# Up projection in one-bank PSUM tiles, with the next pair's seven products set among the last three up tiles

## The chip, the cores and the metric

The kernel runs on one core of one Trainium2 chip. The metric is the device time of one execution in microseconds (us); lower is better. All matrix products are float32 products made of three float32r (fp32r) products: every weight tile is cast to a high part `whi`, and the rest `wlo` is what the cast left; the left operand is split in the same way.

## The reference, cut to what matters

One decoder layer on x of 256 tokens by 2048 features: RMSNorm, two token mixers and an output projection, then a gated MLP. Only the MLP's first product and what follows it are touched:

```python
h = rmsnorm(x, norm_ffn_w[l])
gate, up = jnp.split(jnp.einsum('bsd,df->bsf', h, w_up[l]), 2, axis=-1)   # w_up: 2048 x 11264
gate = causal_dwconv(gate, conv_ffn_w[l]) + conv_ffn_b[l]                  # 3 taps over the tokens
x = x + jnp.einsum('bsf,fd->bsd', jax.nn.gelu(gate, approximate=False) * up, w_down[l])
return rmsnorm(x, norm_final_w)
```

## The kernel before, in words

**The up projection (the loop over c at lines 1334 to 1373).** The 5632 gate columns and the 5632 up columns are cut into 11 pairs of 512 columns. A pair c has four quarters of results, each 128 tokens by 512 columns and one PSUM bank large: `bank[col, t]`, col 0 the gate and 1 the up columns, t the half of the tokens. Four banks are taken as two tiles of two banks from the pool `psm`: (0,0) and (1,0) share a tile, (1,1) and (0,1) share the other.

The sum over the 2048 input features goes in eight chunks of 256 (`kp`). A **plain step** (col, kp) loads one weight tile of 256 by 512 and makes 12 matmuls of 128x512 with it: two token halves, two 128-row slices, and three products each (`products`, L1286 to L1290: high by high, low of the left by high, high of the left by low of the weight). Below, g0 to g5 are the plain steps of the gate column of a pair in the order of kp, u0 to u5 those of the up column. Pair 0 has eight of each. In pairs 1 to 10 the first two chunks are left to a **seven-product scheme** (Strassen's in Winograd's form) over 2x2 blocks: `split_parts` (L1298 to L1328) makes the products T1, 11, T2, 21, T3, 22, T4 of six matmuls each in place of eight. T1 goes into a bank `y` of its own and is copied to SBUF as `own` (L1317); 11 goes into (0,1) and is copied into (0,0) (L1319); T2 is added to (0,1); VectorE writes (1,0) = (0,1) + own (L1322); 21 is added to (0,0); T3 is added to (0,1); VectorE writes (1,1) = (0,1) + own (L1326); 22 is added to (1,0) and T4 to (0,1). Then the plain steps add to all four.

**Order before.** Pair c begins with its seven products; between them stand the transposes of pair c-1's results (`turned`, L332, eight for the gate, eight for the up half, into tiles of `psg`). Then come the plain steps in the order g0, g1, u0, g2, u1, g3, u2, g4, u3, g5, u4, u5. A scheduler that the framework runs at build time may move instructions on every engine within what the data allow.

**Weights.** `weights()` (L158) hands out the next tile and calls `begin` (L231) for the third one after it: the DMA on SyncE's queue (L170, four buffers `raw`), the cast on ScalarE (`whi`, L244) and the rest on VectorE (`wlo`, L252, "the split" below). `whi` and `wlo` have three buffers, so the cast of a tile waits for the last matmul that reads the high part three tiles back. For the seven products four quarter tiles are loaded into the buffer `quad` (`quad_load`, L184, at the earliest when the last pair's T4 has been split) and combined in place on VectorE (`up_sum`, L190: one sum ahead of T1, one behind the split of T1, two behind that of T2).

**What follows a pair.** ScalarE copies the four quarters to SBUF (`e`, L1366 for the gate with a scale, L1368 for the up half), TensorE transposes them, and `gate_part` (L1249: ScalarE L1256, eight VectorE instructions L1261, Gelu L1265) and `up_part` (L1269: L1274, L1281, L1282) run beside the first plain steps of the next pair. `tc.issue_after` keeps the work of `gate_part` behind the named instruction in the engine's order.

**The last pair and the down projection.** In pair 10 no quarters are loaded any more; the residual is read back into the buffer of the quarters, 2 MB from ScalarE's queue (L1377), and the final norm's weights (L1379); `half_sums` (L1228) prepares the first of three seven-product chunks of the down projection, which follows at line 1410.

Of the kernel before, what the change touches and what calls it, by code (L numbers as in the profile page):

```python
# [18 lines left out]
KD = D // P  # L19
# [16 lines left out]
def kernel(  # L36
# [44 lines left out]
    srcs = []  # L81
# [13 lines left out]
    NUP = DFF // 512  # L95
    FOUR = 0
    UP_PARTS = ("T1", "11", "T2", "21", "T3", "22", "T4")
    up_w = [(cols(w_up[0], 512 * c, KD), cols(w_up[0], DFF + 512 * c, KD)) for c in range(NUP)]
    up_steps = []
    for c in range(NUP):  # L100
        kps = [kp for kp in range(KD // 2) if c == 0 or kp // 2 != FOUR]
        order = [(0, kps[0])]
        for a, b in zip(kps[1:], kps):
            order += [(0, a), (1, b)]
        order.append((1, kps[-1]))
        if c:
            srcs += [("up", c, what) for what in UP_PARTS]
        srcs += [up_w[c][col][kp] for col, kp in order]
        up_steps.append(order)
    down = [cols(w_down[0], 512 * c, KF) for c in range(4)]  # L110

    SEVEN = (8, 9, 10)
# [39 lines left out]
    loads = []  # L152
# [117 lines left out]
    def pm():  # L270
        return psm.tile([P, 2, 512], F32, tag="m", name=nm("psm"))
# [52 lines left out]
    def turned(src):  # L324

        out = []
        for f2 in range(2):
            pt = pg([P, 2, S])
            for ff in range(2):
                f = 2 * f2 + ff  # L330
                for t in range(2):
                    nc.tensor.transpose(pt[:, ff, t * P : (t + 1) * P], src[:, t, f * P : (f + 1) * P], ident)  # L332
            out.append(pt)
        return out
# [914 lines left out]
    def gate_part(c, pts):  # L1249

        y = fp.tile([P, 4, S], F32, tag="y", name=nm("y"))
        for f in range(4):
            r = 4 * c + f
            pt = pts[f // 2][:, f % 2, :]
            with tc.issue_after(last_copy[0]) if c < NUP - 1 else ExitStack():
                nc.scalar.activation(y[:, f, :], pt, AF.Identity, scale=cfw[:, 2 * KF + r : 2 * KF + r + 1],  # L1256
                                     bias=vec[:, V_CB + r : V_CB + r + 1])
            with tc.issue_after(last_quad_split[0]) if c < NUP - 1 else ExitStack():
                for j in (1, 0):
                    s = 2 - j  # L1260
                    nc.vector.scalar_tensor_tensor(y[:, f, s:], pt[:, : S - s], cfw[:, j * KF + r : j * KF + r + 1],  # L1261
                                                   y[:, f, s:], op0=ALU.mult, op1=ALU.add)
# [23 lines left out]
    def products(ps, high, low, w, first, last, cs=slice(0, 512), shared=False):  # L1286
        for kk in range(2):
            for n, (part_, lhs) in enumerate(((w[0], high), (w[0], low), (w[1], high))):
                mm(ps[:, cs], lhs(kk), part_[:, kk, cs], start=(first and kk == 0 and n == 0),  # L1289
                   stop=(last and kk == 1 and n == 2), skip_group_check=shared)  # L1290
# [7 lines left out]
    def split_parts(c):  # L1298

        ups = up_ups[0]  # L1300
        bank = banks_of[c]
        y = pg()

        def part(what, ps, first):
            w = weights()
            if what in ("11", "21", "T4"):
                j, t = {"11": (0, 0), "21": (1, 0), "T4": (1, 1)}[what]
                high, low = (lambda kk, f=f: f(4 * FOUR + 2 * j + kk, t) for f in (fh, fl))
            else:
                n = {"T1": 0, "T2": 1, "T3": 2, "22": 3}[what]  # L1310
                high, low = (lambda kk, s=s: s[:, n, kk * P : (kk + 1) * P] for s in ups)
            products(ps, high, low, w, first, False, shared=True)

        chain_ = bank[0, 1]
        part("T1", y, True)
        own = cpool.tile([P, 512], F32, tag="sqj", name=nm("own"))
        nc.scalar.copy(own, y)  # L1317
        part("11", chain_, True)
        last_copy[0] = nc.scalar.copy(bank[0, 0], chain_).ins  # L1319
        yield  # L1320
        part("T2", chain_, False)
        nc.vector.tensor_tensor(bank[1, 0], chain_, own, op=ALU.add)  # L1322
        part("21", bank[0, 0], False)
        yield
        part("T3", chain_, False)
        nc.vector.tensor_tensor(bank[1, 1], chain_, own, op=ALU.add)  # L1326
        part("22", bank[1, 0], False)
        part("T4", chain_, False)  # L1328

    last_copy = [None]  # L1330
    banks_of = {}
    up_ups = []
    pending = []
    for c in range(NUP):
        pair = [pm(), pm()]
        banks_of[c] = {(0, 0): pair[0][:, 0], (1, 0): pair[0][:, 1], (1, 1): pair[1][:, 0], (0, 1): pair[1][:, 1]}
        bank = banks_of[c]
        if c:
            parts = split_parts(c)
            next(parts)  # L1340
            gates = gate_part(c - 1, turned(pending[0]))
            next(parts)
            ups = turned(pending[1])
            for _ in parts:
                pass
        steps_ = up_steps[c]
        left = len(steps_)
        pending = []
        for n, (col, kp) in enumerate(steps_):
            left -= 1  # L1350
            w = weights()
            for t in range(2):
                products(bank[col, t], lambda kk: fh(2 * kp + kk, t), lambda kk: fl(2 * kp + kk, t), w,
                         c == 0 and kp == 0, not any(q[0] == col for q in steps_[n + 1 :]), shared=True)
            if c and n < 3:
                next(gates) if n < 2 else up_part(c - 1, ups)
            if c + 1 < NUP:
                if left in (8, 7, 6, 5):
                    quad_load(c + 1, 8 - left)
                if left == 4:  # L1360
                    up_sum("T1")
            if not any(q[0] == col for q in steps_[n + 1 :]):
                e = fp.tile([P, 2, 512], F32, tag=("eg", "eu")[col], name=nm("e"))
                for t in (0, 1) if col == 0 else (1, 0):
                    if col == 0:
                        nc.scalar.activation(e[:, t, :], bank[col, t], AF.Copy, scale=rs2[:, t : t + 1])  # L1366
                    else:
                        nc.scalar.copy(e[:, t, :], bank[col, t])  # L1368
                pending.append(e)
            if c == 0 and n == 8:  # L1370
                up_ups.append(up_sums())
            if c == NUP - 1 and n == 5:
                half_sums(SEVEN[0])

    xt = fp.tile([P, 2, D], F32, tag="xt", name="xt")
    for c in range(4):
# [33 lines left out]
    for hf in range(2):  # L1410
        if hf == 0:
            own = [pm() for c in range(2)]
            own = {(c, t): own[c][:, t] for c in range(2) for t in range(2)}
            other = [pg() for n in range(4)]
        else:
            own = {(c, t): pg() for c in range(2) for t in range(2)}
            other = [p[:, t] for p in (pm(), pm()) for t in range(2)]
        bank_of = dict(zip(("11", "T1", "T2", "T3"), other))
        bank_of |= {"21": own[0, 0], "22": own[1, 0], "T4": own[0, 1]}
        began = set()  # L1420
        for n, step in enumerate(steps[hf]):
            if hf == 0 and n == 1:
                for _ in gate_part(NUP - 1, turned(pending[0])):
                    pass
            if hf == 0 and n == 2:
                up_part(NUP - 1, turned(pending[1]))
            w = weights()
            if step[0] == "keep":
                wk.append(w)
# [1 line left out]
            if step[0] == "plain":  # L1431
# [128 lines left out]
```

## Time and profile before

| what | value |
|---|---|
| median of 3 runs | 1579.7 us (1578.58 to 1579.83) |
| the profiled execution: its time | 1579.41 us |
| the profiled execution: its span | 1577.5 us |
| granted TensorE clock over the span | 0.997 |
| TensorE matmul busy | 1550.1 us (98%) |
| VectorE busy | 1188.9 us (75%) |
| ScalarE busy | 826.1 us (52%) |
| HBM traffic over the span | 196 GB/s |
| the up projection | from 817 to 1333 us of the span |

The span is the time from the first to the last instruction that the profiler saw; the execution's own time is 1.9 us longer. PE is TensorE, DVE is VectorE, ACT is ScalarE, SP is SyncE, PEld is the weight load of TensorE, which runs beside its matmuls. "Busy" counts an engine as busy while an instruction is in it; matmuls overlap in the pipeline, so a busy TensorE can still be late, and the pace of starts says more than the busy share.

### The profile page before, as it was taken

The page shows a single profiled execution, that of the slowest core. Times are in us where ns is not written, and L with a number is a line of the kernel's source. Part 1 is how long each engine was busy: PE and PEld are TensorE (multiplying, and loading weights), DVE is VectorE, ACT ScalarE, POOL GpSimd, SP SyncE. Part 2 cuts the span into 40 slices and gives each one's busy share as a digit, 9 for nine tenths or more (in the row PEclk, how much of TensorE's full clock was granted, in tenths as well). Part 3 has the DMA queues.
Part 4 walks back from the last instruction along what each step waited for, and adds up shares of the span by engine and source line. Part 5 has one row for each costly group of instructions (what it writes and reads, how often), then busy time and mean ns, then how long its engine had stood idle before and what let it go on. Part 6 is the DMA issues. An engine that isn't in the chain of part 4 may idle for free.

```text
span 1577.5 us, 20038 instructions
## 1 busy us (share of the span) xinstructions
PE 1550.1 (98%) x7350; PEld 1264.2 (80%) x7350; DVE 1188.9 (75%) x1712; ACT 826.1 (52%) x1038; POOL 45.1 (3%) x54
## 2 busy tenths in 40 slices
PE   9999999999999999999999999999999999999998
PEld 8878888888878888888888777777877777788786
DVE  6689858995789859886755777776677775977785
ACT  7455445544545445454554556555555555555552
POOL 1010001000100000000000000000000000000000
PEclk9999999999999999999999999999999999999999
DMA  8777757776676657665775655545665547456562
GB/s 274 209 223 212 195 167 231 208 203 169 187 236 201 193 165 249 186 199 160 250 228 190 214 186 176 174 153 166 214 211 178 173 143 279 165 187 226 188 213 93
DMA packets 168016, 310.45 MB, mean 197 GB/s; under 512 B 19266, under 2 KB 23138, under 8 KB 167790
## 3 DMA queue, kind: packets, MB, share of 16 engines
q1 hardware_dynamic: 162720, 299.95, 60.9%
q10 hardware_dynamic: 5198, 9.23, 1.8%
q8 instruction: 57, 0.93, 0.2%
q14 instruction: 41, 0.34, 0.1%
HBM read 301.75 MB, written 7.38 MB: 196 GB/s over the span
## 4 chain that ended last, share of the span: by engine, by line
PE 89%; DVE 5%; DMA 2%; ACT 2%; issue 2%; POOL 0%; POOLq 0%; ACTq 0%; DVEq 0%
PE psm L1289 32%; PE psm L289 15%; PE psm L287 15%; PE psm L288 14%; PE psg L1289 7%; DVE wlo L252 2%; ACT whi L244 2%; PE psm L430 1%; DVE quad L190 1%; PE psg L332 1%; PE psg L820 1%; DMA raw<-in_w_up_dram 1%; DVE psm L1322 0%; DMA raw<-in_w_down_dram 0%; DVE psm L1326 0%
## 5 line engine op out<-in xcount | busy, mean ns | idle before, releaser
L244 ACT CAST whi<-raw 128x1024 fp32r<-128x1024 f32 x460 | 482.4, 1052 | 514.9 <-PE psm L288 278.4
L252 DVE TENSOR_TENSOR wlo<-raw,whi 128x1024 fp32r<-128x1024 f32 x458 | 557.2, 1221 | 223.7 <-ACT whi L244 221.1
L1289 PE MATMUL psm<-whi,fhl 128*128 128x512 f32 x1208 | 363.7, 396 | 14.9 <-DVE psm L1322 9.7
L289 PE MATMUL psm<-wlo,xhl 128*128 128x512 f32 x864 | 339.5, 393 | 0.7 <-DVE wlo L252 0.7
L287 PE MATMUL psm<-whi,xhl 128*128 128x512 f32 x864 | 338.6, 392 | 0.0
L288 PE MATMUL psm<-whi,xhl 128*128 128x512 f32 x864 | 337.9, 391 | 0.0
L1289 PEld LDWEIGHTS psm<-whi,fhl 128*128 128x128 f32 x1208 | 222.4, 188 | 75.0 <-DVE psm L1322 14.0
L1289 PE MATMUL psm<-wlo,fhl 128*128 128x512 f32 x604 | 218.1, 391 | 0.0
L289 PEld LDWEIGHTS psm<-wlo,xhl 128*128 128x128 f32 x864 | 162.3, 188 | 34.8 <-DVE wlo L252 1.5
L288 PEld LDWEIGHTS psm<-whi,xhl 128*128 128x128 f32 x864 | 162.2, 188 | 33.6
L287 PEld LDWEIGHTS psm<-whi,xhl 128*128 128x128 f32 x864 | 162.2, 188 | 33.2 <-issue 0.2
L252 DVE TENSOR_TENSOR wlo<-quad,whi 128x1024 fp32r<-128x1024 f32 x112 | 136.0, 1222 | 62.6 <-ACT whi L244 62.2
L244 ACT CAST whi<-quad 128x1024 fp32r<-128x1024 f32 x112 | 116.8, 1053 | 77.9 <-PE psm L1289 55.2
L1289 PEld LDWEIGHTS psm<-wlo,fhl 128*128 128x128 f32 x604 | 113.7, 188 | 25.0 <-DVE wlo L252 0.8
L1289 PE MATMUL psm<-wlo,hhi 128*128 128x512 f32 (+1 forms) x150 | 57.9, 388 | 1.6 <-DVE wlo L252 1.6
L1289 PE MATMUL psm<-whi,hhi 128*128 128x512 f32 (+1 forms) x150 | 58.2, 388 | 0.0
L1289 PE MATMUL psm<-whi,hlo 128*128 128x512 f32 (+1 forms) x150 | 58.0, 386 | 0.0
L1289 PE MATMUL psg<-whi,hhi 128*128 128x512 f32 (+1 forms) x130 | 50.3, 387 | 1.7 <-ACT whi L244 1.7
L287 PE MATMUL psm<-whi,mhi 128*128 128x512 f32 x128 | 50.8, 397 | 0.0
L190 DVE TENSOR_TENSOR quad<-quad 128x1024 f32<-128x1024 f32 x40 | 48.8, 1221 | 2.3 <-DMA quad<-in_w_up_dram 1.9
L1289 PE MATMUL psg<-whi,hlo 128*128 128x512 f32 (+1 forms) x130 | 50.2, 386 | 0.0
L289 PE MATMUL psm<-wlo,mhi 128*128 128x512 f32 x128 | 50.0, 390 | 0.0
(331 smaller groups left out, 1713.8 us busy)
## 6 DMA issues: line engine op xcount, KB each, us to landing
raw<-in_w_in_dram SPq DMA_DIRECT2D x224, 512.0 KB, 4.3
raw<-in_w_up_dram SPq DMA_DIRECT2D x136, 512.0 KB, 4.7
raw<-in_w_down_dram SPq DMA_DIRECT2D x64, 512.0 KB, 4.7
quad<-in_w_up_dram SPq DMA_DIRECT2D x40, 512.0 KB, 6.5
raw<-in_w_out_dram SPq DMA_DIRECT2D x32, 512.0 KB, 3.9
quad<-in_w_down_dram SPq DMA_DIRECT2D x12, 1024.0 KB, 6.6
mv<-vrow SPq DMA_DIRECT2D x12, 512.0 KB, 4.6
taps<-in_conv_qkv_w_dram SPq DMA_DIRECT2D x16, 256.0 KB, 6.4
```

The source lines that it names most:

```text
L190: nc.vector.tensor_tensor(out_, plus_, minus_, op=ALU.subtract)
L244: nc.scalar.copy(hi, raw)
L252: last_split[0] = nc.vector.tensor_tensor(lo, raw, hi.bitcast(F32), op=ALU.subtract).ins
L287: mm(ps[:, t, :], lh(k, t), hi[:, kk, :], start=(k == 0), stop=False)
L288: mm(ps[:, t, :], ll(k, t), hi[:, kk, :], start=False, stop=False)
L289: mm(ps[:, t, :], lh(k, t), lo[:, kk, :], start=False, stop=(k == nk - 1))
L332: nc.tensor.transpose(pt[:, ff, t * P : (t + 1) * P], src[:, t, f * P : (f + 1) * P], ident)
L430: mm(ps_k0[:, t, :], part(k, t), w[:, kk, :], start=(k == 0 and w is hi and part is xh), stop=(k == KD - 1 and w is lo))
L820: mm(pg0, kq[:, h, 0, 0:P], kq[:, h, :, :], start=True, stop=True)
L1289: mm(ps[:, cs], lhs(kk), part_[:, kk, cs], start=(first and kk == 0 and n == 0), stop=(last and kk == 1 and n == 2), skip_group_check=shared)
```

## The change

Four things, all in the up projection, and one behind it:

1. **One-bank tiles.** Every quarter is a tile of its own from `psg` (four buffers of one bank, taken in the order (0,1), (0,0), (1,0), (1,1)). T1's bank and the transposes' tiles come from `psm` instead (T1 one, each set of eight transposes one tile of two banks).
2. **Order of the steps.** The plain steps of a pair go g0, g1, g2, g3, u0, g4, u1, g5, u2; u3, u4 and u5 are set among the next pair's products: T1, u3, 11, u4, T2, u5, 21, the gate transposes, T3, 22, the up transposes, T4; then g0 of the next pair. The last pair ends with u3, u4, u5.
3. **Products in written order.** TensorE's order in the whole up projection is the written one (`manual_schedule`); before, the scheduler set it.
4. **High parts first.** `high_first` makes all matmuls of a tile that read `whi` (8 of 12, or 4 of 6), then those that read `wlo`.

Behind it, the first four banks of the down projection are taken from `psg` when each is first written, and `gate_part`'s VectorE instructions stand behind the pair's last sum (`last_sum`) where they stood behind T4's split. Matmuls, transposes, casts, splits, sums and bytes are the same in number.

```diff
+    TAIL = 3
     for c in range(NUP):
         kps = [kp for kp in range(KD // 2) if c == 0 or kp // 2 != FOUR]
-        order = [(0, kps[0])]
-        for a, b in zip(kps[1:], kps):
-            order += [(0, a), (1, b)]
-        order.append((1, kps[-1]))
+        gate_steps, up_only = ([("plain", c, col, kp) for kp in kps] for col in range(2))
+        up_steps += gate_steps[:TAIL]
+        for a, b in zip(gate_steps[TAIL:], up_only):
+            up_steps += [a, b]
+        rest = up_only[-TAIL:]
+        if c + 1 == NUP:
+            up_steps += rest
+            break
+        t1, p11, t2, p21, t3, p22, t4 = [("part", c + 1, what) for what in UP_PARTS]
+        up_steps += [("loads", c + 1)]
+        up_steps += [t1, rest[0], p11, rest[1], t2, rest[2], p21, ("gate", c), t3, p22, ("up", c), t4]
...
-            with tc.issue_after(last_quad_split[0]) if c < NUP - 1 else ExitStack():
+            with tc.issue_after(last_sum[0]) if c < NUP - 1 else ExitStack():
...
+    def high_first(uses, w, first=False):
+        for n in range(2):
+            for kk in range(2):
+                for ps, high, low in uses:
+                    for lhs in (high, low) if n == 0 else (high,):
+                        mm(ps, lhs(kk), w[n][:, kk], start=(first and n == 0 and kk == 0 and lhs is high), stop=False,
+                           skip_group_check=True)
+
+    def up_product(c, what):
+        bank = banks_of.setdefault(c, {})
...
+        w = weights()
+        if what == "T1":
+            bank["own"] = pm()[:, 0]
+        elif what == "11":
+            bank[0, 1] = pg()
+        elif what == "21":
+            bank[1, 0] = pg()
+            last_sum[0] = nc.vector.tensor_tensor(bank[1, 0], bank[0, 1], bank["own"], op=ALU.add).ins
+        ps = {"T1": "own", "21": (0, 0), "22": (1, 0)}.get(what, (0, 1))
+        high_first([(bank[ps], high, low)], w, what in ("T1", "11"))
+        if what == "T1":
+            own = cpool.tile([P, 512], F32, tag="sqj", name=nm("own"))
+            nc.scalar.copy(own, bank["own"])
+            bank["own"] = own
+        elif what == "11":
+            bank[0, 0] = pg()
+            last_copy[0] = nc.scalar.copy(bank[0, 0], bank[0, 1]).ins
+        elif what == "T3":
+            bank[1, 1] = pg()
+            last_sum[0] = nc.vector.tensor_tensor(bank[1, 1], bank[0, 1], bank["own"], op=ALU.add).ins
...
+    def turned_pair(e):
+        both_ = pm()
...
-        pair = [pm(), pm()]
-        banks_of[c] = {(0, 0): pair[0][:, 0], (1, 0): pair[0][:, 1], (1, 1): pair[1][:, 0], (0, 1): pair[1][:, 1]}
...
+    pe_order.enter_context(tc.manual_schedule(engines={mybir.EngineType.PE}))
+    for i, step in enumerate(up_steps):
...
+        for n in range(4):
+            if i + 8 - n < len(up_steps) and up_steps[i + 8 - n][0] == "loads":
+                quad_load(up_steps[i + 8 - n][1], n)
+        if i + 3 < len(up_steps) and up_steps[i + 3][0] == "loads":
+            up_sum("T1")
+    pe_order.close()
...
-            other = [pg() for n in range(4)]
+            other = None
...
+            if what not in bank_of:
+                bank_of[what] = pg()
```

More of the change, by code (lines that the diff above doesn't have):

```diff
@@ L1296, in fl @@
         return both(fhl, k)[:, 1, t * P : (t + 1) * P]
[L1298 to L1308, printed above, removed]
-            else:
[L1310 to L1328, printed above, removed]
@@ new lines, in up_plain @@
+    def up_plain(c, col, kp):
+        bank = banks_of.setdefault(c, {})
+        for t in (1, 0) if col == 0 else (0, 1):
+            if (col, t) not in bank:
+                bank[col, t] = pg()
+        uses = [(bank[col, t], lambda kk, t=t: fh(2 * kp + kk, t), lambda kk, t=t: fl(2 * kp + kk, t)) for t in range(2)]
+        high_first(uses, weights(), c == 0 and kp == 0)
+        if kp == KD // 2 - 1:
+            e = fp.tile([P, 2, 512], F32, tag=("eg", "eu")[col], name=nm("e"))
+            if col == 0:
+                for t in (1, 0):
+                    nc.scalar.activation(e[:, t, :], bank[col, t], AF.Copy, scale=rs2[:, t : t + 1])
+            else:
+                for t in (0, 1):
+                    nc.scalar.copy(e[:, t, :], bank[col, t])
+            pending[c, col] = e
@@ L1330 @@
+    def turned_pair(e):
+        both_ = pm()
+        out_ = [both_[:, f2].rearrange("p (f s) -> p f s", f=2) for f2 in range(2)]
+        for f in range(4):
+            for t in range(2):
+                nc.tensor.transpose(out_[f // 2][:, f % 2, t * P : (t + 1) * P], e[:, t, f * P : (f + 1) * P], ident)
+        return out_
     last_copy = [None]
+    last_sum = [None]
     banks_of = {}
     up_ups = []
-    pending = []
-    for c in range(NUP):
-        pair = [pm(), pm()]
-        banks_of[c] = {(0, 0): pair[0][:, 0], (1, 0): pair[0][:, 1], (1, 1): pair[1][:, 0], (0, 1): pair[1][:, 1]}
[L1337 to L1370, printed above, removed]
@@ L1371 @@
                 up_ups.append(up_sums())
-            if c == NUP - 1 and n == 5:
+            if step[1] == NUP - 1 and step[2:] == (0, KD // 2 - 1):
                 half_sums(SEVEN[0])
+            if work:
+                next(work[0], None)
+        for n in range(4):
[3 more added lines that the diff above has]
+            up_sum("T1")
```

42 lines of the change are left out of this document (34 added, 8 removed).

## The prediction

> **What bounds the kernel now.** The page comes first: the engines' busy shares and the chain that ended last.
>
> ```profile
> span 1577.5 us, 20038 instructions
> ## 1 busy us (share of the span) xinstructions
> PE 1550.1 (98%) x7350; PEld 1264.2 (80%) x7350; DVE 1188.9 (75%) x1712; ACT 826.1 (52%) x1038; POOL 45.1 (3%) x54
> ...
> PE 89%; DVE 5%; DMA 2%; ACT 2%; issue 2%; POOL 0%; POOLq 0%; ACTq 0%; DVEq 0%
> ```
>
> TensorE is the bound, and the change takes no matmul from it. So all there is to win is time in which TensorE does not start a matmul when it could. How much that is in the up projection comes from two views: the windows (one for each pair, cut where T2 starts; columns: stretch, its length, busy of PE, PEld, DVE, ACT, POOL, granted clock, DMA share, GB/s) and the pace of an undisturbed stretch in TensorE's timeline.
>
> ```profile
> 817.40:866.70 49.30, 49.30 (x229) 40.54 (x227) 27.86 (x28) 25.34 (x33) 0.70 (x1) 1.00 0.67 214
> 866.70:913.00 46.30, 45.28 (x203) 36.20 (x202) 33.85 (x37) 28.00 (x33) 0.00 (x0) 1.00 0.55 182
> ...
> 1237.10:1283.40 46.30, 45.31 (x204) 36.20 (x202) 33.84 (x37) 26.66 (x33) 0.00 (x0) 1.00 0.56 182
> 1283.40:1333.10 49.70, 43.84 (x183) 33.82 (x182) 31.78 (x38) 24.51 (x29) 0.00 (x0) 0.97 0.69 241
> ```
>
> ```profile
> 1213.33 1.07 PE L1289 MATMUL psm<-whi,fhl 128*128 128x512 f32 x4
> ...
> 1216.05 1.07 PE L1289 MATMUL psm<-whi,fhl 128*128 128x512 f32 x4
> ```
>
> ```profile
> 1234.29 0.82 PE L332 MATMUL psg<-ident,e 128*128 128x128 f32 x6
> 1234.87 0.71 PE L1289 MATMUL psm<-whi,fhl 128*128 128x512 f32 x2
> ```
>
> The two middle rows are one plain step apart: 12 matmuls in 2.72 us, 0.2267 us each. Six transposes take 0.58 us; with the matmul behind them, which starts late, I take 0.11 each. A pair has 12 plain steps of 12 and seven products of 6, 186 matmuls, and 16 transposes: 186 x 0.2267 + 16 x 0.11 = 42.16 + 1.76 = 43.9 us. The nine regular pairs take 46.3, so each loses 2.4. The last stretch holds 174 matmuls and 8 transposes, 40.3 us, and takes 49.7: it loses 9.4. The first (204 matmuls, about 24 transposes, 48.9 us) loses 0.4. Together 31.4 us: no more can be won in this stage. The waits say on whom TensorE waits: the first row is TensorE in the nine regular pairs, the next four its weight load there, the last two TensorE in the last stretch (us in total, times, longest).
>
> ```profile
> PE psm L1289 <- DVE psm L1322: 7.8, 9, 0.9
> ```
> ```profile
> PEld psm L1289 <- DVE psm L1322: 11.7, 9, 1.3
> PEld psm L1289 <- DVE psm L1326: 5.2, 9, 0.6
> PEld psm L1289 <- ACT whi L244: 3.9, 9, 0.4
> PEld psm L1289 <- ACT e L1366: 2.7, 9, 0.3
> ```
> ```profile
> PE psm L1289 <- ACT whi L244: 3.9, 2, 2.1
> PE psm L1289 <- DVE psm L1322: 1.9, 1, 1.9
> ```
>
> Per regular pair the weight load waits 1.3 + 0.58 + 0.43 + 0.3 us, about the 2.4 that is lost. The causes stand in the VectorE rows below.
>
> **The change part by part.** Durations first (groups of the regular pairs, then rows of one pair's timeline and SyncE's queue):
>
> ```profile
> L252 DVE TENSOR_TENSOR wlo<-quad,whi 128x1024 fp32r<-128x1024 f32 x64 | 77.5, 1222 | 40.7 <-ACT whi L244 40.7
> L190 DVE TENSOR_TENSOR quad<-quad 128x1024 f32<-128x1024 f32 x36 | 43.9, 1221 | 0.3
> L1261 DVE SCALAR_TENSOR_TENSOR y<-psg,cfw,y 128x255 f32<-128x255 f32 (+1 forms) x72 | 32.8, 476 | 0.0
> ```
> ```profile
> L244 ACT CAST whi<-quad 128x1024 fp32r<-128x1024 f32 x63 | 65.3, 1052 | 25.8 <-PE psm L1289 25.8
> ...
> L1368 ACT COPY e<-psm 128x512 f32<-128x512 f32 x18 | 10.4, 580 | 13.3 <-PE psm L1289 13.3
> ```
> ```profile
> 1192.68 0.70 DVE L1322 TENSOR_TENSOR psm<-psm,own 128x512 f32<-128x512 f32 x1
> 1203.12 1.22 DVE L190 TENSOR_TENSOR quad<-quad 128x1024 f32<-128x1024 f32 x1
> ```
> ```profile
> 1193.43 0.73 PE L1289 MATMUL psm<-whi,fhl 128*128 128x512 f32 x2 [0.86 <-DVE psm L1322]
> ```
> ```profile
> 1197.27 1.91 SPq L184 DMA_DIRECT2D quad<-in_w_up_dram  x4
> ```
>
> *One-bank tiles.* 21 adds to (0,0), but waited for the write of (1,0), its tile's other bank: the sum L1322 ends at 1193.38, 21 starts at 1193.43. As tiles of their own they have nothing to do with each other. The wait of 0.3 on the copies `e` goes for the same reason.
>
> *Products among plain steps.* Before, the stretch of seven products (42 matmuls, 16 transposes: 11.3 us) asks VectorE for 7 splits of 1.22, 3 sums of 1.22 and two of 0.70, 13.6 us: VectorE cannot keep up there. Over T1 to T4 with u3 to u5 it is 19.4 us of TensorE against 17.3. The casts gain too: a cast waits for the tile three back, and with plain steps between products that is 4.1 us ahead, not 2.7.
>
> *High parts first.* The low part is read 8 matmuls into a plain step (1.8 us) and not at the third, and `whi` comes free three matmuls earlier. Nothing is added.
>
> *What is late next.* One wait is new: the bank for (1,0) is now a buffer of `psg` that held the previous pair's up quarter, so its sum (L1322's successor) must follow the copy `e`, which follows u5; T3, which overwrites what the sum reads, waits for the sum. From the start of u5's eighth matmul, after which the cast for 22 may begin: cast from about 0.44 to 1.49 (matmul 0.39, hand-over 0.05, cast 1.05), on ScalarE behind it the two copies to 2.07 and 2.65; on VectorE, in the changed order, first 22's split, 1.54 to 2.76, then the sum to 3.46; T3 may start at 3.51. TensorE gets there after 5 matmuls of u5, 21's six and eight transposes: 2.49 + 0.88 = 3.4. So T3 is late by about 0.1, with the late weight load I take 0.25 per pair. Bounds: 0, and 1.15 if the cast had to wait for u5's last matmul (4 x 0.2267 later). Behind the sum on VectorE stand T4's split and the second sum; T4's split would end about 2 us before T4, so they bear it. The second sum (behind T3) ends about 1.1 us ahead of T4. The quarters' DMAs, behind g3's load on SyncE, wait for T4's split as before, but that is now 3.3 us ahead of T4's end, where it was about 0.5; so the first sum of the next pair, early in VectorE's order, keeps its cover.
>
> Nine pairs: 9 x (2.4 - 0.25) = **19.4 us**. First stretch: **0.3** of its 0.4.
>
> *Last pair.* Two of its long waits are the regular ones made longer by `half_sums`, whose first instruction (1.22 us) stood ahead of L1322's sum; in the changed order it stands behind both sums. The third is another matter:
>
> ```profile
> 1306.82 1.04 ACT L244 CAST whi<-raw 128x1024 fp32r<-128x1024 f32 x1 [8.33 <-DMA raw<-in_w_up_dram]
> ```
> ```profile
> 1307.91 1.21 PE L1289 MATMUL psm<-whi,fhl 128*128 128x512 f32 x4 [2.13 <-ACT whi L244]
> ```
> ```profile
> 1295.10 6.47 SPq L170 DMA_DIRECT2D raw<-in_w_up_dram  x4
> ```
> ```profile
> 1309.80:1313.20 3.40, 3.40 (x9) 2.23 (x8) 2.23 (x3) 2.79 (x3) 0.00 (x0) 0.50 0.56 157
> ```
>
> The load issued at 1295.1, behind 2 MB of residual, lands 11.7 us later; TensorE idles 2.13 us, and right behind it runs 3.4 us at half clock, 1.7 us more. In the changed order the residual's DMAs start with T4's split, 3.3 us ahead of T4's end, and the load in question about 2 us behind them: it comes in time or nearly, the next one perhaps 0.6 late. The half clock follows idle time here (0.86 us idle in a regular pair leaves the clock at 1.00). [...] I leave 1.65 us lost of the 9.4 (0.25 at T3, 1.4 at the loads; bounds 0 and 4.4, stall and half clock both kept): **7.7 us**.
>
> *Start of the down projection.* The scheduler had moved the last gate transposes ahead of the first down step; now they stand behind it, 2.7 us later. Of the eight instructions L1261 the second half then falls behind `whole` into a stretch where VectorE has no idle time:
>
> ```profile
> 1340.30 1.23 DVE L1235 TENSOR_TENSOR whole<-hhi,hlo 128x1024 f32<-128x1024 f32 x1 [0.46 <-PE psg L332]
> ```
> ```profile
> 1350.60 0.50 PE L1289 MATMUL psm<-wlo,hhi 128*128 128x512 f32 x1 [1.64 <-DVE wlo L252]
> ```
>
> That stretch already ends in a stall of 1.64; four more of 0.476 make up to 1.9 us more. I take **-1.4** (bounds 0 and -4, a longer stall with half clock).
>
> Sum: 19.4 + 0.3 + 7.7 - 1.4 = 26.0 us. The profiled execution, 1579.4 (its span 1577.5 and 1.9 around it), becomes 1553.4; the median stands 0.3 above it: **1553.7 us**.
>
> **The rivals.** *New waits keep half.* T3 late by its bound of 1.15 in nine pairs (8.1 less), the last pair's stall and half clock kept (2.7 less), the down start at -3 (1.6 less): a gain of 13.6, 1566.1. For it: T3's margin is a tenth of a microsecond on two engines' orders. Against: every step of the walk uses measured durations.
>
> *Slower: the quarters land too late.* VectorE's changed order has the first sum of the next pair right behind g1's split and one L1261, with the splits of g2 and g3 behind it. g2's low part is needed 10.5 us after the quarters' issue (3.3 ahead of T4's end, two steps, 1.8); sum, one L1261 and split take 2.9, so a landing later than 7.6 us costs TensorE the difference in ten pairs. From 10.2 us on the whole gain is gone; at the 11.7 us of the load above it is 4.1 x 10 = 41 us lost, 1594.7. Against: before, that sum started at 1203.12, 5.85 us after the issue, without waiting.
>
> [...]
>
> *It does not do what it says.* If 21 keeps waiting for the sum through some other tie, the plain steps only move: 1577 to 1582.
>
> **How the numbers follow.** Forecast 0.70, new waits 0.17, quarters late 0.06, clock 0.04, no effect 0.03. The forecast's own range is 1548 (all 31.4 us won) to 1561 (T3 at 0.6, last pair at its bound). To hold 8 in 10 the range takes in the first rival: 1548 to 1567. About 0.2% is what a measurement of this kernel can tell from no change. Faster by more: 0.70 + 0.17 + 0.04 = 0.91; within it 0.03; slower 0.06.
>
> **What would show it.** Right: windows of about 44.1 us per pair; no wait of TensorE on the first sum at 21; a short one at T3; the last stretch near 42 us at clock 1.00. Wrong: a wait on VectorE's sum at T3 over 0.5 us; VectorE waiting for the quarters' DMA ahead of a split; a clock below 1.00 in regular pairs; more idle time than before at the start of the down projection.

## The result, and the profile after

The changed kernel takes **1553.4 us** (median of 4 runs, 1552.89 to 1555.58) against 1579.1 beside it on the same chip (4 runs, 1578.23 to 1579.83): a ratio of 0.984, interval 0.9823 to 0.9857. The forecast was 1553.7 us. The medians differ by 25.7 us. The span of the profiled execution fell from 1577.5 to 1551.2 us, by 26.3; it is these 26.3 that are divided by stages below.

The page of the changed kernel, its first lines and the shares of the chain of waits by engine:

```profile
span 1551.2 us, 20085 instructions
## 1 busy us (share of the span) xinstructions
PE 1538.3 (99%) x7350; PEld 1267.7 (82%) x7350; DVE 1195.5 (77%) x1712; ACT 827.5 (53%) x1038; POOL 44.7 (3%) x54
...
PE 93%; DMA 3%; DVE 2%; issue 1%; ACT 1%; POOL 0%; POOLq 0%; DVEq 0%; ACTq 0%
```

The matmuls are the same 7350, and VectorE is as busy as before (1195.5 us against 1188.9): no work went. VectorE's share of the chain that ended last fell from 5 to 2%: it is time in which TensorE waited that went. (TensorE's busy time fell too, by 11.8 us, with the same matmuls: a row of one matmul of 128x512 counts 0.39 us as busy, while the next starts after 0.2267 where nothing is late, so short late starts are hidden in the busy time.) Where it went, the windows say, cut again where T2 starts (the columns are those of the windows of before):

```profile
820.70:870.70 50.00, 50.00 (x227) 41.45 (x225) 30.88 (x31) 26.47 (x34) 0.70 (x1) 1.00 0.61 201
870.70:914.80 44.10, 44.10 (x204) 36.60 (x202) 34.41 (x37) 28.14 (x33) 0.00 (x0) 1.00 0.57 191
...
1223.40:1267.50 44.10, 44.10 (x205) 36.60 (x202) 34.50 (x37) 26.98 (x32) 0.00 (x0) 1.00 0.58 191
1267.50:1310.00 42.50, 41.91 (x192) 34.16 (x190) 28.76 (x35) 23.43 (x28) 0.00 (x0) 1.00 0.83 288
```

A regular pair takes 44.1 us in place of 46.3, and TensorE is busy in all of it. The last pair has lost its half clock (1.00; it was 0.97 over the stretch).

By stages of the span, before and after (the marks are starts of TensorE's first matmul of the up and of the down projection):

| stage | before | after | difference |
|---|---|---|---|
| up to the first up matmul | 817.4 | 820.8 | +3.4 |
| up projection | 515.8 | 485.7 | -30.0 |
| down projection to the end | 244.3 | 244.7 | +0.4 |

Some of this is bookkeeping: eight transposes of the residual x (0.88 us) moved from behind the first up matmuls to ahead of them, and eight transposes of the last gate columns from ahead of the first down matmul to behind it. Like for like the up projection gained 28.3 us. Of the 3.4 us ahead of it, 0.88 are these transposes, 1.48 a new gap (below), and 1.0 lie earlier, where TensorE's matmuls stand in the same order. That much varies between executions: in the five later kernels that have neither these transposes nor the gap ahead of the first up matmul it came at 818.0, 818.2, 818.9, 819.3 and 819.4 us (e9, e12, e11, e10, e7).

### The profile page after: what moved, and what is told of

Its sections match the earlier page's. It is cut to its first block, busy times and chain, and to the rows that moved or that the text cites. A ratio compares the mean times of both kernels' runs of the same rounds, so it can differ in the third digit from the quotient of the medians.

```text
span 1551.2 us, 20085 instructions
## 1 busy us (share of the span) xinstructions
PE 1538.3 (99%) x7350; PEld 1267.7 (82%) x7350; DVE 1195.5 (77%) x1712; ACT 827.5 (53%) x1038; POOL 44.7 (3%) x54
## 4 chain that ended last, share of the span: by engine, by line
PE 93%; DMA 3%; DVE 2%; issue 1%; ACT 1%; POOL 0%; POOLq 0%; DVEq 0%; ACTq 0%
PE psg L1313 28%; PE psm L298 14%; PE psm L296 14%; PE psm L297 14%; PE psm L1298 7%; PE psg L1298 5%; PE psm L439 1%; PE psm L1370 1%; PE psg L341 1%; DVE wlo L261 1%; PE psm L1313 1%; DMA vrow<-ev 1%; DMA raw<-in_w_up_dram 1%; PE psg L829 1%; ACT whi L253 1%
## 5 line engine op out<-in xcount | busy, mean ns | idle before, releaser
L261 DVE TENSOR_TENSOR wlo<-raw,whi 128x1024 fp32r<-128x1024 f32 x458 | 556.4, 1220 | 174.0 <-ACT whi L253 167.1
L1313 PE MATMUL psg<-whi,fhl 128*128 128x512 f32 x1208 | 302.1, 390 | 0.6 <-ACT whi L253 0.6
L1313 PEld LDWEIGHTS psg<-whi,fhl 128*128 128x128 f32 x1208 | 225.8, 188 | 47.7 <-ACT whi L253 1.4
L261 DVE TENSOR_TENSOR wlo<-quad,whi 128x1024 fp32r<-128x1024 f32 x112 | 137.1, 1224 | 73.0 <-ACT whi L253 71.8
L1313 PE MATMUL psg<-wlo,fhl 128*128 128x512 f32 x604 | 164.0, 389 | 0.0
L1313 PEld LDWEIGHTS psg<-wlo,fhl 128*128 128x128 f32 x604 | 113.4, 188 | 23.6
```

What stands on the lines that cost most here:

```text
L261: last_split[0] = nc.vector.tensor_tensor(lo, raw, hi.bitcast(F32), op=ALU.subtract).ins
L1313: mm(ps, lhs(kk), w[n][:, kk], start=(first and n == 0 and kk == 0 and lhs is high), stop=False, skip_group_check=True)
```

## The experiments

Beside each run ran the kernel before; times are medians, and a pair is the distance of the starts of T1, a mean over the nine regular pairs. "One-bank tiles", "order", "written order" and "high parts first" are the four parts of the change. The changed kernel ran once more as a yardstick (e5): 0.9834 of the time before.

**e1, one-bank tiles alone.** Order of the steps, order of the products and TensorE's order (left to the scheduler) are those of before; the quarters' loads are started nine steps and the first sum five steps ahead of the products, where the changed kernel has eight and three.

```diff
...
-        up_steps += [t1, rest[0], p11, rest[1], t2, rest[2], p21, ("gate", c), t3, p22, ("up", c), t4]
+        up_steps += [t1, p11, ("gate", c), t2, p21, ("up", c), t3, p22, t4]
...
-    pe_order.enter_context(tc.manual_schedule(engines={mybir.EngineType.PE}))
...
```

> One part alone, the one-bank tiles (steps in the order of before, TensorE's order left to the scheduler, products tile half by tile half as before). Theory (false ties through shared tiles cost 1.0 us at 21 and some tenths elsewhere in each pair, VectorE's load in the seven products the rest): 21 no longer waits for VectorE's sum, a regular pair takes 45.0 to 45.6 us in place of 46.3, the kernel 1566 to 1572. Rival (VectorE is late in this stretch anyway, the wait moves to T3 or 22): a pair stays above 46.0, the kernel above 1575.

Measured: 1562.7 us, ratio 0.9887 (0.9872 to 0.9902); a pair takes 44.88, under the range of the theory. So 1.4 of the 2.2 us won per pair come from the tiles alone. What TensorE's weight load still waits for in the pairs (time in total, times, longest):

```profile
PEld psg L1311 <- ACT psg L1339: 8.0, 10, 0.8
PEld psg L1311 <- DVE wlo L260: 0.5, 1, 0.5
```

That is T2 waiting for ScalarE's copy of 11 (L1339 here). A split is late in one pair of ten (0.5 us), and none of them waits at 21: the gain is larger than the prediction's reasoning gives to the ties alone, and what is left is not VectorE's load.

**e2, everything but the order of the steps.** Steps as in e1's diff; one-bank tiles, written order and high parts first as changed.

> The changed kernel with the step order undone: the seven products stand together again at the start of a pair, gate and up steps alternate as before; one-bank tiles, written order and high parts first stay. Theory (VectorE needs 13.6 us in a stretch of 11.3, so putting plain steps among the products is worth about half of the gain): a regular pair takes 45.1 to 45.7 us, the kernel 1563 to 1569, with TensorE waiting for splits. Rival (the tiles, the written order and high parts first are enough): a pair within 0.4 us of 44.1, the kernel below 1558.

Measured: 1561.8 us, 0.9883 (0.9866 to 0.9899), a pair 44.74: between the theory (45.1 to 45.7) and the rival (under 44.5). The wait is e1's again, and no split is late in the regular pairs. ScalarE's timeline around it, and TensorE's rows (start, length, instruction, count, then the idle time ahead and what ended it):

```profile
1223.80 1.06 ACT L252 CAST whi<-quad 128x1024 fp32r<-128x1024 f32 x1
1224.75 0.59 ACT L1336 COPY own<-psm 128x512 f32<-128x512 f32 x1
1225.22 1.06 ACT L252 CAST whi<-quad 128x1024 fp32r<-128x1024 f32 x1
1226.17 0.60 ACT L1340 COPY psg<-psg 128x512 f32<-128x512 f32 x1
```
```profile
1224.82 0.63 PE L1312 MATMUL psg<-wlo,fhl 128*128 128x512 f32 x2
1225.28 1.04 PE L1369 MATMUL psm<-ident,e 128*128 128x128 f32 x8
1226.83 1.19 PE L1312 MATMUL psg<-whi,ups 128*128 128x512 f32 x4 [0.51 <-ACT psg L1340]
```

11 ends at 1225.45, but its copy stands behind a cast on ScalarE and ends at 1226.77; the eight transposes are too short a cover. In the changed order u4, twelve matmuls, stands between 11 and T2. So, with the tiles split, the order of the steps is worth 0.65 us a pair, by this cover. The theory that it relieves VectorE falls, and so does its size, about half of the gain: it is 0.65 of 2.2.

**e3, TensorE's order left to the scheduler.** Only the `manual_schedule` line is taken out of the changed kernel.

> The changed kernel with TensorE's order left to the scheduler. Theory (the written order itself is worth little once the waits are gone; the 1.3 us idle ahead of the up projection stays where the scheduler leaves the last transposes in front): 1551 to 1556. Rival (the scheduler moves products against VectorE's order and brings waits back): more than 1 us per pair, above 1563.

Measured: 1556.9 us, 0.9848 (0.9833 to 0.9862), a pair 44.30. In the nine regular pairs the weight load waits for the first sum, at T3:

```profile
PEld psg L1313 <- DVE psg L1332: 2.0, 9, 0.2
```

The written order is worth 0.2 us a pair (44.30 against 44.09).

**e4, the old order of the products within a weight tile.** The rest as changed.

```diff
-        for n in range(2):
-            for kk in range(2):
-                for ps, high, low in uses:
-                    for lhs in (high, low) if n == 0 else (high,):
+        for ps, high, low in uses:
+            for kk in range(2):
+                for n, lhs in ((0, high), (0, low), (1, high)):
```

> The changed kernel with the products of a tile in the order of before (high, low, high by low for each slice), nothing else. Theory (high parts first matters because the high part comes free three matmuls earlier, 0.68 us: without it the cast for 22, its split and the sum behind it end that much later, and T3 waits): TensorE waits for the first sum about 0.5 to 0.7 us in each of ten pairs, 44.7 to 44.9 us a pair, the kernel 1558 to 1562. Rival 1 (low parts come late: TensorE waits for splits instead, 1 us a pair or more): above 1563. Rival 2 (nothing depends on it): within 1.5 us of 1553.4.

Measured: 1551.8 us, 0.9815 (0.9801 to 0.983), a pair 43.96 and no late start at T3. The theory expected a slower kernel; it is, if anything, faster: high parts first buys nothing here. Why, the timelines show. In the changed kernel ScalarE, VectorE and TensorE (its rows are 21 and T3):

```profile
1220.52 1.05 ACT L253 CAST whi<-quad 128x1024 fp32r<-128x1024 f32 x1 [1.21 <-PE psg L1313]
1221.48 1.06 ACT L1361 COPY e<-psg 128x512 f32<-128x512 f32 x2
```
```profile
1221.61 1.23 DVE L261 TENSOR_TENSOR wlo<-quad,whi 128x1024 fp32r<-128x1024 f32 x1 [1.04 <-ACT whi L253]
1222.75 0.69 DVE L1332 TENSOR_TENSOR psg<-psg,own 128x512 f32<-128x512 f32 x1
```
```profile
1221.23 1.07 PE L1313 MATMUL psg<-whi,fhl 128*128 128x512 f32 x4
...
1223.50 1.19 PE L1313 MATMUL psg<-whi,ups 128*128 128x512 f32 x4
```

and in e4 ScalarE and VectorE:

```profile
1218.98 0.59 ACT L1360 COPY e<-psg 128x512 f32<-128x512 f32 x1 [0.53 <-PE psg L1312]
1220.12 1.05 ACT L253 CAST whi<-quad 128x1024 fp32r<-128x1024 f32 x1 [0.55 <-PE psg L1312]
1221.07 0.58 ACT L1360 COPY e<-psg 128x512 f32<-128x512 f32 x1
```
```profile
1219.63 0.69 DVE L1331 TENSOR_TENSOR psg<-psg,own 128x512 f32<-128x512 f32 x1
```

High parts first goes to and fro between the two quarters of u5, so both are finished with its last matmuls. The old order finishes the first quarter six matmuls (1.36 us) earlier; its copy `e` goes ahead of the cast for 22, the bank for (1,0) comes free, and the sum is written ahead of 22's split, with 2 us to spare at T3. In the changed kernel the sum ends at 1223.44 and T3 starts at 1223.50; 21 starts 1.5 us ahead of the sum, which it no longer waits for.

**e5, the changed kernel again**, the yardstick of the next three.

> The changed kernel as it is, a yardstick for the kernels that run beside it on the same chip. Expected: 0.9835 to 0.985 of the time before, 1.48 us of late start ahead of the up projection, loads late by 1.1 us in the last pair, nothing lost in the regular pairs but 0.2 us at T3.

Measured: 1552.6 us, 0.9834 (0.9821 to 0.9848), a pair 44.1, 1.48 late ahead of the up projection. In the last pair late casts cost 0.33 us, in place of 0.92 in the first profile (1.1 with the matmul behind each), and a cast in the down projection near 1466 us that waits for its load cost 1.87 in place of 0.92: these two differ by 0.6 and 0.95 us between executions of one kernel.

**e6, products ordered by quarter**, high parts first within each.

```diff
-        for n in range(2):
-            for kk in range(2):
-                for ps, high, low in uses:
+        for ps, high, low in uses:
+            for n in range(2):
+                for kk in range(2):
```

> The changed kernel with the products of a weight tile ordered by quarter: all six matmuls of the first quarter (high parts first within it), then all six of the second. Theory from the run with the old product order: what helps there is that a quarter is finished 6 matmuls (1.36 us) before the other, so the first copy e stands ahead of the cast for 22, the bank for (1,0) comes free and its sum is written ahead of 22's split, and T3 no longer touches its deadline; whether high or low parts come first within a quarter is of no matter. Then: no wait at T3, pair 43.95 to 44.0, a time 1 to 3 us under the changed kernel beside it. Rival: the product order acts through the low part (needed later or earlier); then this order, with the high parts ahead within a quarter, lies between the two, at a pair of about 44.05, within 0.7 us of the changed kernel.

Measured: 1551.8 us, 0.9828 (0.9814 to 0.9842), a pair 43.96: e4's pair, and no late start at T3. So the early end of a quarter is what counts, not which part comes first. As a time, 0.8 us under e5, it is within the intervals; the pairs show it.

**e7, the last eight transposes of x behind g0**, in the two halves of one tile of `psm`.

```diff
...
             up_plain(*step[1:])
+            if i == 0:
+                both_ = pm()
+                turn_h(3, [both_[:, k2].rearrange("p (k s) -> p k s", k=2) for k2 in range(2)])
...
```

`turn_h(c, pts)` holds the eight transposes of a block c of x and what reads them, which stood in the loop ahead.

> The changed kernel with the last eight transposes of the residual x ahead of the up projection taken into a tile of psm and written behind the first plain step g0. Theory: the 1.48 us that TensorE starts late ahead of the up projection is the wait of these transposes for VectorE's residual add, which before had 12 matmuls set in front of them; with g0 in front (2.72 us) nothing waits, and the time falls by 1.3 to 1.6 us. Rival: the wait comes from the bank that the transposes take (a buffer of psg that is still read); then a tile of psm removes it too, but the first g steps must then wait for their own banks of psg: a late start of 0.5 us or more at the first up matmul stays and the gain is under 0.7 us.

Measured: 1556.3 us, 0.9857 (0.9843 to 0.987), slower than e5. The target of the edit is the row that the changed kernel has ahead of its up projection:

```profile
819.93 1.09 PE L1204 MATMUL psg<-ident,xt 128*128 128x128 f32 x8 [1.32 <-DVE xt L1194]
```

In e7 this wait is gone (first up matmul at 819.42, without a gap), as the theory had it. But a greater one has come, 6 us on:

```profile
822.15 0.60 PE L1194 MATMUL psm<-ident,xt 128*128 128x128 f32 x4
...
824.35 0.47 DVE L1200 SCALAR_TENSOR_TENSOR fhl<-psm,vec,fhl 128x256 fp32r<-128x256 f32 x1
...
825.37 0.48 DVE L1200 SCALAR_TENSOR_TENSOR fhl<-psm,vec,fhl 128x256 fp32r<-128x256 f32 x1 [0.47 <-ACT fhl L1199]
...
825.90 1.11 PE L1194 MATMUL psm<-ident,xt 128*128 128x128 f32 x4 [3.15 <-DVE fhl L1200]
```
```profile
825.55:828.96 3.41, 3.06 (x10) 2.58 (x11) 1.15 (x3) 0.95 (x2) 0.12 (x1) 0.50 0.73 190
```

The second four transposes start right behind VectorE's last read of the first four, though they write another bank. It looks like the tie that the change removed, made anew by the edit, and 3.4 us at half clock follow.

**e8, the reload of the residual later** (behind the last copy `e`), in the changed kernel.

```diff
...
+    with tc.issue_after(last_e[0]):
+        for c in range(4):
+            nc.scalar.dma_start(xt[:, :, c * 512 : (c + 1) * 512], xt_d[:, :, c * 512 : (c + 1) * 512])
+        nc.scalar.dma_start(nfin, norm_final_w.partition_broadcast(P))
...
```

> The changed kernel with the reload of the residual (2 MB) and of the final norm's weights issued behind the last copy e of the last pair in place of the start of that pair. Theory: the late casts in the last pair (0.58 and 0.34 us, with the matmul behind each 1.1 us together) are weight loads behind these 2 MB; with the reload later they go, and the time falls by 0.9 to 1.3 us, if the down projection's own loads bear the 2 MB. Rival: the loads are late for the quarters (the last 4 MB before them) or for the buffers of raw, and the late casts stay; or the 2 MB hit the down projection's loads and a stall of 1 to 2 us with half clock turns up there: same or slower by up to 4 us.

Measured: 1553.3 us, 0.9835 (0.9822 to 0.9849): the same as e5. The late casts of the last pair are gone, but a wait of 0.47 has come at 1319 us and the cast near 1466 is late by 2.19 us. Whether the reload pushes these or they fell so is open; nothing is won.

**e9, two-bank tiles in the new order.** Only the tiles go back.

```diff
...
-            bank[0, 1] = pg()
+            both_ = pm()
+            bank[0, 0], bank[0, 1] = both_[:, 0], both_[:, 1]
...
-            bank[1, 0] = pg()
+            both_ = pm()
+            bank[1, 0], bank[1, 1] = both_[:, 0], both_[:, 1]
...
```

> The changed kernel with two-bank tiles again: the two gate quarters of a pair share a tile of psm, the two up quarters share the other, T1's bank and the transposes go back to psg; order, written order and high parts first stay. Theory (the new order is worth something only because the tiles are split): 21, which adds to (0,0), waits for VectorE's sum that reads (0,1) in its tile, and 22, which adds to (1,0), waits for the sum that writes (1,1). In the changed kernel the first sum ends 2.2 us after 21's start and the second 0.9 us after 22's: 2.2 to 3.3 us lost in each of ten pairs, 1575 to 1587 us. Rival (the new order itself hides the sums, and the split tiles are a detail): under 0.8 us lost per pair, a time under 1563.

Measured: 1587.6 us, 1.0046 (1.0033 to 1.0059): **slower than the kernel before**. In the pairs TensorE and its weight load wait for the two sums:

```profile
PE psm L1313 <- DVE psm L1334: 18.9, 9, 2.1
PE psm L1313 <- DVE psm L1344: 8.0, 9, 0.9
```

Late by 2.27 us at 21 and 1.05 at 22 in each pair, 3.3 together, the upper end of what was worked out; the time lies 0.6 us above its range, with 3.4 us at half clock in two of the pairs (last section). The two parts are not to be added: tiles alone win 17.8 us of 1580 (e1), the rest without the tiles loses 7.3, both together win 26.

**e10, e7's edit with the two sets in two tiles.**

```diff
-                both_ = pm()
-                turn_h(3, [both_[:, k2].rearrange("p (k s) -> p k s", k=2) for k2 in range(2)])
+                turn_h(3, [pm()[:, 0].rearrange("p (k s) -> p k s", k=2) for k2 in range(2)])
```

> The run with the late transposes of x once more, with its two sets of four transposes in two tiles in place of the halves of one. Theory: the 3.15 us there were the wait of the second set for VectorE's reads of the first set, in the other bank of the same tile, and the 3.4 us at half clock came of that idle time; with two tiles both go, what is left is the gain at the start: 1.3 to 1.6 us under the changed kernel, about 1551. Rival: the second set waits for VectorE or ScalarE themselves, which are behind there (the tile is a second reason only): a wait of over 1 us stays at the second set, and the time is at or above that of the changed kernel.

Measured: 1552.1 us, 0.9823 (0.981 to 0.9835), 4.2 us under e7. TensorE at the place where e7 waited:

```profile
819.31 1.98 PE L1317 MATMUL psg<-whi,fhl 128*128 128x512 f32 x8
821.12 1.08 PE L1317 MATMUL psg<-wlo,fhl 128*128 128x512 f32 x4
822.04 1.03 PE L1194 MATMUL psm<-ident,xt 128*128 128x128 f32 x8
822.83 2.07 PE L1317 MATMUL psg<-whi,fhl 128*128 128x512 f32 x8
```

Eight transposes in one go, no wait, no half clock (the eight matmuls behind them take 2.07 us, in e7 3.15): the wait in e7 was the shared tile and nothing else. Against e5 the ratio falls by 0.0011, 1.7 us, as expected; the intervals overlap, so the size rests on the profile, where the 1.48 are gone.

**e11, e6's and e10's edits together.**

> Both changes that were worth something, together: products ordered by quarter, and the last transposes of x behind g0 in two tiles. If the two add, 0.13 x 10 and 1.4 us: 2.5 to 3 us under the changed kernel, about 1549 to 1550. Rival: what is won ahead of the up projection and in the pairs is given back in the down projection, whose late cast near 1466 us varied between 0.9 and 2.2 us from run to run: same as the changed kernel within its interval.

Measured: **1550.8 us**, 0.9814 (0.9801 to 0.9826), a pair 43.96, no gap ahead of the up projection. It beats the kernel before plainly; against the changed kernel's 0.9834 it is 3 us, the size that was expected, with intervals that still touch.

**e12, the kernel before with the reload later**, e8's edit.

> The kernel before, with the reload of the residual and of the final norm's weights issued behind the last copy e. Theory (of the prediction): the 2.13 us of idle time and the 3.4 us at half clock behind it (1.7 us more) in the last pair come from weight loads behind these 2 MB, and the half clock from the idle time; both go, the clock of the stretch is 1.00, and the time falls by 3.5 to 4 us, to about 1575.5; the two waits on VectorE in that stretch stay. Rival 1: the half clock comes of something else in that stretch (the banks, the two waits on VectorE): the idle time goes and the half clock stays, 2 us won. Rival 2: the loads are late for the quarters of the pair itself, nothing changes.

Measured: 1575.9 us, 0.9977 (0.9967 to 0.9987), ten executions between 1573.7 and 1579.9. The last pair's window:

```profile
1283.40:1329.00 45.60, 42.27 (x189) 33.81 (x188) 32.04 (x39) 24.82 (x28) 0.00 (x0) 1.00 0.60 196
```

The 2.13 us of idle time are gone and the half clock with them, while the two waits on VectorE's sums stay (1.9 and 1.4 us; before, the second was 1.8 and ended with a cast of ScalarE, whose queue also issues the reload). The medians differ by 3.8 us, which is the theory's figure. The half clock went with the idle time (1.00 over the window in place of 0.97), and the idle time with the early reload.

## Why the prediction was right, point by point

- **One-bank tiles: right, and more than it said.** 21 no longer waits for the sum. e1 and e9 show the tie on both sides: without it 17.8 us are won in the old order, with it 34 are lost again in the new (1.0046 against 0.9834). The prediction left part of this to the order.
- **Products among plain steps: right that it helps, the reason wrong.** "VectorE cannot keep up there" did not hold: with the tiles split and the old order, one split in ten pairs is late by 0.5 us (e1), and none in e2. The order is worth 0.65 us a pair because u4 covers ScalarE's copy of 11 ahead of T2.
- **Nine pairs, 19.4 us: measured 20.0** (46.31 to 44.09 each). The ideal pair of 43.9 stood up: e4 and e6 come to 43.96.
- **T3 late by 0.25: measured 0.13** (44.09 against 43.96 in e4, where nothing waits there). The walk had T3 touch the sum, and it does: the sum ends at 1223.44, T3 starts at 1223.50. The rival in which this wait is 1.15 failed.
- **High parts first, "nothing is added": wrong, by these 0.13 us a pair.** Both quarters of u5 end together, which brings the sum behind 22's split (e4, e6). The walk to T3 had this order in it and so its number right; the sentence on what the order costs was wrong.
- **First stretch and last pair, 0.3 and 7.7: measured 8.3 together** (28.3 less 20.0). The loads came late by 1.1 us (forecast 1.4; in e5 a third of that). That the half clock goes with the idle time was the author's estimate from one stretch of the kernel before (2.13 us idle, then 3.4 at half clock); the changed kernel's last stretch has the clock at 1.00, and in e12 both went from the kernel before.
- **Start of the up projection: not in the prediction, -1.5.** The scheduler now sets the last transposes of x ahead of the first up matmul, where they wait for VectorE's add. Before, they stood 3.2 us behind it and did not wait:

```profile
820.60 1.03 PE L1195 MATMUL psg<-ident,xt 128*128 128x128 f32 x8
```

  e1 and e3 have the same gap with the scheduler's order, so it isn't the written order of the up projection that puts them there; in e9, which has two-bank tiles, they stand at 823.7, behind two plain steps, and don't wait. It comes with the one-bank tiles from `psg`, the pool of these transposes; by what rule the scheduler decides was not tried. e10 removes it. The diff does not touch these lines, but TensorE's order in the changed kernel could have been read ahead of the run, and was not at this place.
- **Start of the down projection, -1.4: measured about 0.** The stall of 1.80 us at 1350.6 became four of 0.60, 0.27, 0.27 and 0.17, and behind each of the long ones the next matmul, too, starts after 0.34 us in place of 0.23. From the first down matmul to the one that has 799 matmuls and transposes behind it in both kernels it takes 58.40 us before and 59.24 after, and 0.88 of that are the eight transposes that moved in. Like for like the whole stage still won 0.5, but further on, at casts that wait for the down projection's loads: 1.85 us at 1493 before, 0.92 at 1466 and 0.40 at 1488 after; e5 shows how these vary. The prediction moved the second half of L1261's instructions to behind `whole`, which is what happened, but did not move what stands behind them. VectorE's timeline there, before and in the changed kernel:

```profile
1342.58 1.28 DVE L1274 TENSOR_TENSOR y<-psg,y 128x512 f32<-128x512 f32 x2
...
1347.05 1.22 DVE L1282 TENSOR_TENSOR hlo<-y,hhi 128x1024 fp32r<-128x1024 f32 x1
...
1349.33 1.22 DVE L252 TENSOR_TENSOR wlo<-raw,whi 128x1024 fp32r<-128x1024 f32 x1
```

```profile
1313.93 1.22 DVE L1244 TENSOR_TENSOR whole<-hhi,hlo 128x1024 f32<-128x1024 f32 x1 [0.86 <-PE psg L341]
...
1318.80 0.86 DVE L1270 SCALAR_TENSOR_TENSOR y<-psg,cfw,y 128x254 f32<-128x254 f32 x2
...
1322.18 1.22 DVE L261 TENSOR_TENSOR wlo<-raw,whi 128x1024 fp32r<-128x1024 f32 x1
1323.32 1.28 DVE L1283 TENSOR_TENSOR y<-psg,y 128x512 f32<-128x512 f32 x2
...
1327.12 1.22 DVE L1291 TENSOR_TENSOR hlo<-y,hhi 128x1024 fp32r<-128x1024 f32 x1
```

  The split that TensorE waits for (L252 before, L261 after) now stands ahead of `up_part`'s instructions (1.28 and 1.22 us), which stood ahead of it before; 1.7 us of L1270 came in and 2.5 went out.
- **The quarters land too late: seen, and free.** VectorE does wait for them:

```profile
1230.46 1.23 DVE L199 TENSOR_TENSOR quad<-quad 128x1024 f32<-128x1024 f32 x1 [1.16 <-DMA quad<-in_w_up_dram]
```

  The quarters were issued from 1224.78; the sum waits 1.16 us in this pair, 4.4 us in all nine, and no matmul for it. The rival's margin (a landing after 7.6 us) was used up to within 2 us, not passed.
- **The clock, 0.04 of the chances:** no run shows a half clock that comes with the change of banks. The granted clock is 1.00 in all regular pairs, with banks changing every one or two matmuls.

So the sum of 26.0 against 26.3 is better than its terms, and in that part luck: the start of the down projection, 1.4 us better than its term, paid for the start of the up projection (1.5 us, no term); the pairs and the last stretch came out 0.9 us better, and 0.5 us went where executions vary (1.0 lost ahead of the up projection, 0.5 won at late casts). What made the forecast good are the two large terms, and these came from lost time counted against a measured pace. One bound of the prediction does not add up: T3 at 0.6 and the last pair at its bound make 1559.6 us, not 1561; nothing hangs on it.

## What to carry to other kernels

Where an engine waits for an instruction that touches none of its data, look whether the two share a tile: here a tile of two banks tied banks that had nothing to do with each other, worth 18 us in one order and 34 in another. An edit of the order and an edit of the tiles are to be tried together and apart, since either alone can have the other sign. And of the products of one weight tile, those that free a buffer which the next step needs are to be finished first, ahead of any preference for which part is read first.

## What the runs showed of the hardware

Half clock followed idle time of TensorE, but not each time. In e9 every pair has the same wait of 2.1 us, and two of ten are followed by 3.4 us at half clock, the first and the last row here; behind the wait ahead of the middle row the clock stayed at 1.00 (columns as above):

```profile
869.10:872.50 3.40, 3.40 (x12) 2.77 (x11) 0.76 (x1) 1.18 (x2) 0.00 (x0) 0.50 0.00 0
1060.30:1063.70 3.40, 3.29 (x18) 2.82 (x19) 1.02 (x2) 1.97 (x3) 0.00 (x0) 1.00 0.00 0
1108.10:1111.40 3.30, 3.30 (x10) 2.61 (x11) 0.27 (x1) 1.05 (x1) 0.00 (x0) 0.50 0.00 0
```

The length of the wait does not tell the cases apart:

| run | wait of TensorE that ends at | idle us | granted clock, window |
|---|---|---|---|
| before | 1287.10 | 1.91 | 1.00, 1285:1292 |
| before | 1293.26 | 1.77 | 1.00, 1292:1300 |
| before | 1307.91 | 2.13 | 0.50, 1309.8:1313.2 |
| before | 1350.60 | 1.64 | 1.00, 1350.6:1354 |
| e4 | 1465.89 | 1.85 | 0.50, 1466.95:1470.36 |
| e7 | 825.90 | 3.15 | 0.50, 825.55:828.96 |

1.85 us (e4) came with half clock and 1.91 (before) did not; of e9's waits of 2.1 us some did and some did not. Why, the runs do not show. What it costs they do: four matmuls in e4's stretch start 0.43 us apart (1467.79 to 1469.07) in place of 0.2267, and a wait that cost nothing more in one pair of e9 cost 1.6 us more in another (a pair takes 47.5 us without half clock and 49.1 with it).
